# Rotary embedding on one core: six slabs in flight, engine passes of 2048 elements

## Chip, cores and metric

The kernel runs on one core of a Trainium2 chip. The metric is the time of the program on the device in microseconds (us), the median of several runs. Beside it stands one execution taken by the hardware profiler, with its own span from the first to the last instruction.

Five kinds of engine matter here. VectorE (DVE in the profile) does the multiplications and additions, ScalarE (ACT) the conversions between float32 and bf16, TensorE (PE) and GpSimd (POOL) a little preparation. SyncE (SP), ACT and POOL also issue transfers between the memory outside (HBM) and the on-chip memory of 128 partitions. Each of these three has a queue of its own, and all queues are worked off by the core's 16 DMA engines.

## What is computed

The input x has 16 batches of 512 positions with 16 heads of 64 elements. In each head the first 32 elements and the last 32 are rotated against each other by a cosine and a sine of the position (float32 in and out, 33.5 MB each way):

```python
x = x.reshape(batch, seq, num_heads, head_dim)        # 16, 512, 16, 64
x1, x2 = x[..., :half_dim], x[..., half_dim:]
cos = cos[None, :, None, :]                           # cos, sin: 512 x 32
sin = sin[None, :, None, :]
rotated = np.concatenate([x1 * cos - x2 * sin,
                          x1 * sin + x2 * cos], axis=-1)
```

## The kernel before

The work is cut into 8 slabs (`nslabs`) of two batches. A slab is one tile of 128 partitions with 8192 float32 each (8 positions of 1024 elements, `rpp = 8`), 32 KB in a partition and 4 MB in all. One transfer loads it, and one stores it from the same tile. The pool `slabs` has 5 such tiles (`slots`), so a load of slab s + 5 can only start when the store of slab s has landed.

*Loads* (L60 to L64). Slab 0 is issued on SP, then the two tables cos and sin (L73), then slabs 1 to 4. Further loads are issued in the main loop behind the store of the slab whose tile they take: slab 5 still on SP, slabs 6 and 7 on POOL (`s < nslabs - 2` chooses). SP has nothing else to do; POOL has only the preparation at the start, so a wait in front of a load holds up nothing else there.

*Tables* (L80 to L103). GpSimd builds a selection matrix and converts the tables to bf16, four matmuls spread them to 128 partitions, and VectorE copies the result to `tab`: a cosine part, and a sine part with signs.

*Passes.* A pass (s, r, n) is n of the 8 positions of slab s, that is n x 1024 elements in each partition. Slabs 1 to 5 are one pass of 8192 elements, slabs 0, 6 and 7 two passes of 4096. A pass goes through:

1. `cast` (L112): ScalarE copies the float32 slab to the bf16 buffer `xb`. There are two such buffers (`xpool`), each as large as a whole slab in bf16 (16 KB in a partition).
2. VectorE multiplies twice (L133), by the sine part into `t2` and by the cosine part in place. `t2` lies in the slab's own memory, whose float32 values are no longer needed.
3. VectorE adds the two, with the halves of each head exchanged (L136).
4. ScalarE copies the bf16 result back to the slab as float32 (L139).
5. Behind the last pass of a slab ScalarE issues the store (L141).

The loop casts one pass ahead: on ScalarE the cast of pass i + 1 comes in front of the copy back of pass i. An engine works in the order of its instructions, so where that cast waits for a slab still to be loaded, the copy back and the store behind it wait too. The scheduler of the language reorders within this: at the start, it puts the cast of slab 1 in front of both copies back of slab 0, and it interleaves the VectorE operations of the first two passes.

Of the kernel before, what the change touches and what calls it, by code (L numbers as in the profile page):

```python
# [2 lines left out]

# [4 lines left out]


@with_exitstack  # L10
def kernel(
    ctx: ExitStack,
    tc: tile.TileContext,
    x: bass.AP,
    cos: bass.AP,
    sin: bass.AP,
    num_heads: int,
    out: bass.AP,
):
    nc = tc.nc  # L20
    P = nc.NUM_PARTITIONS

    batch, seq, dim = x.shape
    nh = num_heads
    hd = dim // nh
    half = hd // 2
    bf16 = mybir.dt.bfloat16
    f32 = mybir.dt.float32

    nb = 2  # L30
    slots = 5
    nslabs = batch // nb
    rpp = nb * seq // P
    W = rpp * dim
    SP = seq // rpp
    TW = rpp * half

    out_flat = out.rearrange("b s h d -> b s (h d)")

    singles = ctx.enter_context(tc.tile_pool(name="singles", bufs=1))  # L40
    slabs = ctx.enter_context(tc.tile_pool(name="slabs", bufs=slots))
    xpool = ctx.enter_context(tc.tile_pool(name="xpool", bufs=2))
    psum = ctx.enter_context(tc.tile_pool(
        name="psum", bufs=1, space=bass.MemoryType.PSUM))


    def dram(t, s, a=0, n=W):
        return bass.AP(tensor=t.tensor, offset=t.offset + s * nb * seq * dim + a,
                       ap=[[W, P], [1, n]])


    def view(t, offset, *dims):
        return dataclasses.replace(t, offset=t.offset + offset,
                                   ap=[t.ap[0], *[list(d) for d in dims]])


    slab = {}


    def load(s):  # L60

        queue = nc.sync if s < nslabs - 2 else nc.gpsimd
        slab[s] = slabs.tile([P, W], f32, tag="slab", name="slab")
        queue.dma_start(out=slab[s], in_=dram(x, s))  # L64


    load(0)


    cos_sb = singles.tile([SP, TW], f32, tag="cos_sb")  # L70
    sin_sb = singles.tile([SP, TW], f32, tag="sin_sb")
    for t, src in ((cos_sb, cos), (sin_sb, sin)):
        nc.sync.dma_start(out=t, in_=bass.AP(  # L73
            tensor=src.tensor, offset=src.offset, ap=[[TW, SP], [1, TW]]))

    for s in range(1, slots):
        load(s)

    pick = singles.tile([SP, 2 * P], bf16, tag="pick")
    nc.gpsimd.memset(pick, 0.0)  # L82
    for g in range(2):
        part = view(pick, g * P, (SP, P // SP), (1, SP))
        nc.gpsimd.affine_select(  # L85
            out=part, in_=part, compare_op=mybir.AluOpType.not_equal,
            fill=1.0 - 2.0 * g, base=0, pattern=[[0, P // SP], [-1, SP]],
            channel_multiplier=1)

    tab1 = singles.tile([SP, 2 * TW], bf16, tag="tab1")  # L90
    for i, t in enumerate((cos_sb, sin_sb)):
        nc.gpsimd.tensor_copy(out=view(tab1, i * TW, (1, TW)), in_=t)  # L92

    acc = psum.tile([P, 2 * rpp * hd], f32, tag="acc")
    for i in range(2):
        for h in range(2):
            nc.tensor.matmul(  # L97
                view(acc, i * rpp * hd + h * half, (hd, rpp), (1, half)),
                view(pick, i * h * P, (1, P)),
                view(tab1, i * TW, (half, rpp), (1, half)),  # L100
                start=True, stop=True)
    tab = singles.tile([P, 2 * rpp * hd], bf16, tag="tab")
    nc.vector.tensor_copy(out=tab, in_=acc)  # L103

    xb = {}


    def cast(u):
        s, r, n = u
        if r == 0:  # L110
            xb[s] = xpool.tile([P, W], bf16, tag="xb", name="xb")
        nc.scalar.copy(out=view(xb[s], r * dim, (1, n * dim)),  # L112
                       in_=view(slab[s], r * dim, (1, n * dim)))

    passes = []
    for s in range(nslabs):
        n = rpp if 1 <= s < nslabs - 2 else rpp // 2  # L120
        passes += [(s, r, n) for r in range(0, rpp, n)]


    cast(passes[0])
    for i, (s, r, n) in enumerate(passes):
        if i + 1 < len(passes):
            cast(passes[i + 1])
        xs = view(slab[s], r * dim, (1, n * dim))
        xu = view(xb[s], r * dim, (1, n * dim))

        t2 = view(slab[s].bitcast(bf16), 2 * r * dim, (1, n * dim))
        for t, a in ((t2, rpp * hd), (xu, 0)):
            nc.vector.tensor_mul(  # L133
                out=t, in0=xu,
                in1=view(tab, a + r * hd, (hd, n), (0, nh), (1, hd)))
        nc.vector.tensor_add(  # L136
            out=xu, in0=xu, in1=view(t2, half, (hd, n * nh), (-half, 2), (1, half)))

        nc.scalar.copy(out=xs, in_=xu)  # L139
        if r + n == rpp:  # L140
            nc.scalar.dma_start(out=dram(out_flat, s), in_=slab[s])  # L141
            if s + slots < nslabs:
                load(s + slots)


# [1 line left out]
_INS = ['x', 'cos', 'sin', 'num_heads']  # L147
_OUTS = [((16, 512, 16, 64), 'float32')]

_NUMBERS = {'num_heads': 16}  # L150


# [26 lines left out]
```

## Time and profile before

| What | Value |
|---|---|
| Median of 3 runs | 162.46 us (162.06 to 162.85) |
| Span of the profiled execution | 160.2 us |
| DVE busy | 108.6 us (68%) |
| ACT busy | 113.5 us (71%) |
| Bytes moved by DMA | 67.24 MB, mean 420 GB/s over the span |
| Loads on SP | 6, median 26.6 us from issue to landing |
| Loads on POOL | 2, median 24.9 us |
| Stores on ACT | 8, median 25.9 us |

The slices in the profile are fortieths of the span, 4 us each; a digit is the busy share of a slice in tenths, and 9 stands for 90% or more. A line of an instruction group has the source line, the engine, the operation, output and inputs with their shapes, the count; then the busy time and the mean length of one in ns; then the idle time of the engine just before these instructions and what ended it. A line of the timeline has the start, the length, the engine, the source line and the operation; a bracket has the idle time before it and what ended that. An engine named with a q (SPq, ACTq) is its instruction queue: issuing a transfer takes time there and is not counted as busy.

### The profile page before, as it was taken

What the parts mean: (1) busy time and instruction counts of PE and PEld (TensorE: products, weight loads), DVE (VectorE), ACT (ScalarE), POOL (GpSimd) and SP (SyncE); (2) the same over time, 40 slices, a digit from 0 to 9 for tenths busy, and PEclk for the clock granted to TensorE, in tenths of its full rate; (3) what the DMA queues carried; (4) which work ended last, traced back from release to release, by engine and by line L of the source; (5) the groups of instructions that cost most, each with busy time, mean ns of one, the idle gap of its engine ahead of it and who ended that gap; (6) DMA issues with size and microseconds to landing.
All of it is one profiled execution on the core that took longest, in us unless ns stands there. A gap on an engine that the chain in (4) does not pass through costs nothing.

```text
span 160.2 us, 159 instructions
## 1 busy us (share of the span) xinstructions
PE 1.0 (1%) x4; PEld 0.5 (0%) x4; DVE 108.6 (68%) x34; ACT 113.5 (71%) x23; POOL 3.0 (2%) x11
## 2 busy tenths in 40 slices
PE   0002000000000000000000000000000000000000
PEld 0000000000000000000000000000000000000000
DVE  0001899999979979997997299919839499940000
ACT  3006929998999999899919995089995999553000
POOL 2001000000000000000010001000000000000000
DMA  7999999999999999999999999999999999999995
GB/s 246 409 393 426 393 450 466 393 417 491 401 393 426 491 393 409 499 401 393 483 434 393 450 466 393 426 483 401 409 491 409 393 475 442 393 442 475 393 426 229
DMA packets 2464, 67.24 MB, mean 420 GB/s; under 512 B 288, under 2 KB 416, under 8 KB 416
## 3 DMA queue, kind: packets, MB, share of 16 engines
q10 hardware_dynamic: 1152, 33.55, 48.5%
q1 hardware_dynamic: 1024, 25.30, 37.5%
q0 software_dynamic: 288, 8.39, 12.1%
HBM read 33.69 MB, written 33.55 MB: 420 GB/s over the span
## 4 chain that ended last, share of the span: by engine, by line
DMA 49%; ACT 28%; issue 8%; DVE 4%; SPq 1%; ACTq 0%; POOLq 0%
DMA slab<-in_x_dram 29%; DMA out_dram<-slab 20%; ACT slab L139 16%; ACT xb L112 12%; DVE xb L136 1%; DVE xb L133 1%; DVE slab L133 1%; SPq L73 1%; ACTq L141 0%; SPq L64 0%; POOLq L174 0%; ACTq L139 0%; POOLq L64 0%
## 5 line engine op out<-in xcount | busy, mean ns | idle before, releaser
L112 ACT CAST xb<-slab 128x4096 bf16<-128x4096 f32 (+1 forms) x11 | 56.6, 5155 | 27.8 <-DMA slab<-in_x_dram 26.5
L139 ACT CAST slab<-xb 128x4096 f32<-128x4096 bf16 (+1 forms) x11 | 56.6, 5154 | 3.5 <-DVE xb L136 3.5
L133 DVE TENSOR_TENSOR slab<-xb,tab 128x4096 bf16<-128x4096 bf16 (+1 forms) x11 | 35.9, 3260 | 17.3 <-ACT xb L112 17.2
L133 DVE TENSOR_TENSOR xb<-xb,tab 128x4096 bf16<-128x4096 bf16 (+1 forms) x11 | 35.9, 3261 | 0.3
L136 DVE TENSOR_TENSOR xb<-xb,slab 128x4096 bf16<-128x4096 bf16 (+1 forms) x11 | 35.9, 3261 | 0.3
L103 DVE CAST tab<-acc 128x1024 bf16<-128x1024 f32 x1 | 1.2, 1225 | 15.2 <-PE acc L97 15.2
L64 POOL DMA_DIRECT2D slab<-in_x_dram x2 | 1.2, 608 | 84.1 <-DMA out_dram<-slab 84.1
L112 ACT ACT_TABLE_LOAD x1 | 1.3, 1283 | 0.7 <-PEq L160 0.7
L97 PE MATMUL acc<-tab,pick 64*128 64x256 bf16 x4 | 1.0, 402 | 14.2 <-POOL tab L92 14.2
L92 POOL CAST tab<-cos_sb 64x256 bf16<-64x256 f32 x1 | 0.4, 389 | 12.1 <-DMA cos_sb<-in_cos_dram 12.1
L85 POOL TENSOR_SCALAR_AFFINE_SELECT pick<-pick 64x128 bf16<-64x128 bf16 x2 | 0.5, 285 | 0.1
L97 PEld LDWEIGHTS <-pick 64*128 64x128 bf16 x4 | 0.5, 122 | 14.2 <-issue 12.6
L92 POOL CAST tab<-sin_sb 64x256 bf16<-64x256 f32 x1 | 0.4, 394 | 0.0
L82 POOL MEMSET pick<- 64x256 bf16 x1 | 0.3, 304 | 0.3 <-POOLq L160 0.3
L160 POOL MEMSET const-float32-0.0<- 128x1 f32 x1 | 0.1, 103 | 0.2 <-issue 0.2
L160 POOL MEMSET const-bfloat16-1.0<- 128x1 bf16 x1 | 0.1, 107 | 0.0
L160 POOL MEMSET const-uint8-127<- 128x1 uint8 x1 | 0.1, 106 | 0.0
L160 POOL MEMSET const-float32-1.0<- 128x1 f32 x1 | 0.1, 103 | 0.0
## 6 DMA issues: line engine op xcount, KB each, us to landing
out_dram<-slab ACTq DMA_DIRECT2D x8, 4096.0 KB, 25.9
slab<-in_x_dram SPq DMA_DIRECT2D x6, 4096.0 KB, 26.6
slab<-in_x_dram POOLq DMA_DIRECT2D x2, 4096.0 KB, 24.9
cos_sb<-in_cos_dram SPq DMA_DIRECT2D x1, 64.0 KB, 12.5
sin_sb<-in_sin_dram SPq DMA_DIRECT2D x1, 64.0 KB, 12.3
```

Source lines behind the costliest of these rows:

```text
L64: queue.dma_start(out=slab[s], in_=dram(x, s))
L73: nc.sync.dma_start(out=t, in_=bass.AP(tensor=src.tensor, offset=src.offset, ap=[[TW, SP], [1, TW]]))
L82: nc.gpsimd.memset(pick, 0.0)
L85: nc.gpsimd.affine_select(out=part, in_=part, compare_op=mybir.AluOpType.not_equal, fill=1.0 - 2.0 * g, base=0, pattern=[[0, P // SP], [-1 ...
L92: nc.gpsimd.tensor_copy(out=view(tab1, i * TW, (1, TW)), in_=t)
L97: nc.tensor.matmul(view(acc, i * rpp * hd + h * half, (hd, rpp), (1, half)), view(pick, i * h * P, (1, P)), view(tab1, i * TW, (half, rpp) ...
L103: nc.vector.tensor_copy(out=tab, in_=acc)
L112: nc.scalar.copy(out=view(xb[s], r * dim, (1, n * dim)), in_=view(slab[s], r * dim, (1, n * dim)))
L133: nc.vector.tensor_mul(out=t, in0=xu, in1=view(tab, a + r * hd, (hd, n), (0, nh), (1, hd)))
L136: nc.vector.tensor_add(out=xu, in0=xu, in1=view(t2, half, (hd, n * nh), (-half, 2), (1, half)))
L139: nc.scalar.copy(out=xs, in_=xu)
L160: nc = _bacc.Bacc("TRN2", target_bir_lowering=False, num_devices=1)
```

## The change

Three things are changed. The pool has six slab tiles instead of five; slabs 0 to 5 are loaded on SP, 6 and 7 on POOL, which the line that chooses the queue now says with `slots`. The bf16 buffers hold one pass instead of one slab (two of 2048 elements, 4 KB in a partition, in place of two of 16 KB), and are taken anew for each pass. Each of the 8 slabs goes through the engines in four passes of 2048 elements, 32 passes in place of 11.

```diff
-    slots = 5
+    slots = 6
...
     def load(s):
 
-        queue = nc.sync if s < nslabs - 2 else nc.gpsimd
+        queue = nc.sync if s < slots else nc.gpsimd
...
     def cast(u):
         s, r, n = u
-        if r == 0:
-            xb[s] = xpool.tile([P, W], bf16, tag="xb", name="xb")
-        nc.scalar.copy(out=view(xb[s], r * dim, (1, n * dim)),
-                       in_=view(slab[s], r * dim, (1, n * dim)))
+        xb[u] = xpool.tile([P, n * dim], bf16, tag="xb", name="xb")
+        nc.scalar.copy(out=xb[u], in_=view(slab[s], r * dim, (1, n * dim)))
...
     for s in range(nslabs):
-        n = rpp if 1 <= s < nslabs - 2 else rpp // 2
+        n = rpp // 4
         passes += [(s, r, n) for r in range(0, rpp, n)]
...
         xs = view(slab[s], r * dim, (1, n * dim))
-        xu = view(xb[s], r * dim, (1, n * dim))
+        xu = xb[s, r, n]
```

With 32 passes there are 32 casts, 32 copies back and 96 operations on VectorE, where there were 11, 11 and 33. The order on ScalarE is now a strict exchange: cast of pass i + 1, copy back of pass i, with the store issued behind the fourth copy back of a slab. A cast takes the buffer that the copy back just ahead of it has read. The first load in the loop, that of slab 6, waits for the store of slab 0, and that of slab 7 for the store of slab 1; the number and size of all transfers are as before.

## The prediction

> **What bounds the kernel now.** I read the slices and the queue table first, then the windows at both ends, then the instruction groups with shapes kept apart, then the timeline, and last the records that the trace keeps of every DMA packet. The slices and the queue table:
>
> ```profile
> span 160.2 us, 159 instructions
> ...
> DMA  7999999999999999999999999999999999999995
> ...
> q10 hardware_dynamic: 1152, 33.55, 48.5%
> q1 hardware_dynamic: 1024, 25.30, 37.5%
> q0 software_dynamic: 288, 8.39, 12.1%
> ```
>
> Between the first and the last slice the 16 DMA engines never fall below nine tenths, and the three queues (q1 is SP's loads, q10 ACT's stores, q0 POOL's loads) add up to 98.1% of their time. The windows at the ends show where the rest is:
>
> ```profile
> 0.00:2.40 2.40, 0.00 (x0) 0.10 (x1) 0.00 (x0) 1.28 (x1) 1.05 (x7) 1.00 0.72 191
> ...
> 157.00:160.20 3.20, 0.00 (x0) 0.00 (x0) 0.00 (x0) 0.00 (x0) 0.00 (x0) 1.00 0.38 164
> ```
>
> The last two columns are the DMA share and GB/s. So DMA is idle only while the first transfer is set up and while the last store completes. The kernel is bound by 16 slab transfers (8 in, 8 out). A packet is one partition's 32768 bytes, each engine moves 8 of them for a slab, and a packet takes 1.216 us: a slab alone is 8 x 1.216 = 9.73 us, and two queues that are busy together each take 19.4 us for one (the packet records have slab 4's load from 44.1 to 63.5, beside the stores).
>
> The engines are the second limit:
>
> ```profile
> L112 ACT CAST xb<-slab 128x8192 bf16<-128x8192 f32 x5 | 35.1, 7018 | 7.9 <-DMA slab<-in_x_dram 6.6 <-ACT slab L139 1.3
> ...
> L139 ACT CAST slab<-xb 128x4096 f32<-128x4096 bf16 x6 | 21.5, 3602 | 3.5 <-DVE xb L136 3.5
> ...
> L133 DVE TENSOR_TENSOR slab<-xb,tab 128x8192 bf16<-128x8192 bf16 x5 | 22.1, 4425 | 7.3 <-ACT xb L112 7.3
> ...
> L133 DVE TENSOR_TENSOR xb<-xb,tab 128x4096 bf16<-128x4096 bf16 x6 | 13.7, 2291 | 0.2
> ```
>
> The rates fix the short forms. ScalarE: (7018 - 3602) / 4096 = 0.834 ns an element, and 186 ns fixed. VectorE: (4425 - 2291) / 4096 = 0.521 ns an element, and 157 ns fixed. The timeline gives the moments that the change touches:
>
> ```profile
> 13.38 7.11 ACT L112 CAST xb<-slab 128x4096 bf16<-128x4096 f32 x2 [11.37 <-DMA slab<-in_x_dram]
> ...
> 37.60 0.38 ACTq L141 DMA_DIRECT2D out_dram<-slab  x1
> ...
> 79.90 0.69 POOL L64 DMA_DIRECT2D slab<-in_x_dram  x1 [65.41 <-DMA out_dram<-slab]
> ...
> 99.23 0.53 POOL L64 DMA_DIRECT2D slab<-in_x_dram  x1 [18.65 <-DMA out_dram<-slab]
> ...
> 145.54 0.34 ACTq L141 DMA_DIRECT2D out_dram<-slab  x1
> ```
>
> Stores issue about every 14.4 us, the loads of slabs 6 and 7 wait on POOL for the stores of slabs 1 and 2, and the last store issues at 145.5 us while earlier stores still move: its own first packet starts only at 148.9 us, its last ends at 159.2. The engines thus have some 3 us in hand.
>
> **The change, part by part.** *Bytes and transfers* are the same 16 slabs, so the DMA time itself (156.7 us of packets per engine) is neither removed nor shortened. With no idle in the middle, deeper buffering has nothing to fill. The kernel can stay at 160.2 us or lose.
>
> The Trainium skill says the same of queues in "DMA: Bandwidth & Descriptors", Rules for kernel authors: spreading transfers over SP, ACT and GpSimd brings no bandwidth, as all run on the same 16 engines. In this trace SP alone moved 431 GB/s (23 to 37.6 us), and SP and ACT together 433 (60 to 80).
>
> *Shorter passes.* A 2048-element copy is 186 + 2048 x 0.834 = 1.894 us, a multiply or add 157 + 2048 x 0.521 = 1.224. Between them lie 0.02 us (ScalarE behind its own result, read at 51.97 to 51.99), 0.035 (VectorE behind its own), 0.03 (copy to VectorE, 91.23 to 91.26) and 0.05 (VectorE to copy; the one case in the trace is 0.09 with two waits). With two xb buffers the way from one VectorE pass to the second next is: copy out, copy in, three VectorE operations: 0.05 + 1.894 + 0.02 + 1.894 + 0.03 + 3 x 1.224 + 2 x 0.035 = 7.63 us for two passes, 15.25 for a slab. Behind each slab ScalarE also issues a store (0.38 more, on this way): **15.63 us a slab**, against 14.35 now (store issues at 51.99 and 66.34). Bounds: ScalarE's own work, 8 x 1.894 + 0.40 less four overlaps of 0.09 and plus 0.08, is 15.27; with every hand-over at 0.09 the sum is about 16.2.
>
> The Trainium skill, "VectorE: DVE Perf Modes", The TRN2 errata, charges each instruction a fixed part that small tiles pay per tile, 58 cycles at 0.96 GHz for VectorE: an estimate of 1.127 us for this operation. The rows measure 157 ns fixed instead of 60, so the measurement decides; by the page ScalarE would set the period at 15.3 us, and the sum below would end at 160.4 us instead of 161.5.
>
> *First store.* Slab 0 lands at 13.4 and the tables at 16.5, as now. The first two passes are interleaved on VectorE (six operations from 16.5 end at 23.65). On ScalarE: out 0 from 21.3, in 2, out 1 (to 26.9), in 3 (to 28.8), out 2 (28.9 to 30.8), the first piece of slab 1 (landed at 23.8, so no wait; to 32.7), out 3 to 34.6. Store 0 issues at **34.6 us instead of 37.6**, and, if no load is waited for, the last one at 34.6 + 7 x 15.63 = 144.0.
>
> *Six slabs.* SP now issues loads 0 to 5 at once; the wait that goes is this one:
>
> ```profile
> SPq L64 <- DMA out_dram<-slab: 56.7, 1, 56.7
> ```
>
> The sixth load has one wait left, for a semaphore that the cos table used (landed at 13.7 us); its turn in the ring comes 40 us later, so this costs nothing. Loads 6 and 7 stay on POOL, but wait for stores 0 and 1. So where load 6 came after load 5, it now starts while loads 4 and 5 are still queued on SP: a **third busy queue**, which takes its share from the slabs that are needed sooner. By the packet records, step by step:
>
> - Store 0's first packet came 3.7 us after its issue (37.60 to 41.26): now 38.3. Load 2 ends at 33.0 as before, so load 3 is 5.3 us in.
> - Two queues share evenly until store 0 lands: 38.3 + 19.5 + 0.3 = 58.1. From a store's landing to the first packet of the load that it frees on POOL took 5.5 us (79.3 to 84.8; 98.7 to 104.2): load 6 starts at 63.6.
> - By then SP has moved 5.3 + 25.3/2 = 17.95 of the 29.2 us of loads 3 to 5; 11.25 are left. At a third each they take 33.7 us, to 97.3. The other two queues stay busy so long: load 6 takes 29.2 us to 92.8, load 7 is behind it (store 1 lands near 83), and stores 1 to 3 issue at 50, 66 and 81.
> - A slab has landed when the slowest engine is done. In turns of three its last packet can lie up to two packet times (2.4 us) behind the even share; I take 1.2, and 0.3 for the landing: **slab 5 is there at 98.8 us**. Nothing here shows three queues, so: with no loss to the third (SP keeps half) it would be 87.6, with POOL taking half 100.3. I take a third, as the two queues of today share evenly.
>
> Store 4 stands behind slab 5's first copy on ScalarE, and would be ready at 97.1; it now issues at 98.8 + 2 x 1.9 = 102.6. Behind it come three slabs of engine work, 3 x 15.63 = 46.9: the last store issues at 149.5. DMA has nothing else to do from 149.5 on (the other 15 slabs end there), so this is a tail with nothing over it: 1.24 to the first packet (as load 0, 0.74 to 1.98), 9.73 to move, 0.97 to the end of the span (159.18 to 160.15). **Sum: 149.5 + 11.9 = 161.5 us, 1.3 more than 160.2.** The median of the runs, 162.46, lies 2.3 above the profiled span, so 163.8.
>
> The bounds: slowest engine 0 to 2.4 us (-1.2 to +1.2); period 15.27 to 16.2 (-1.1 to +1.7); POOL taking half, +1.5; store 0's first packet only 1.24 us after issue, as on idle engines, which moves load 6 forward and slab 5 to 103.7, +4.9. Downward everything stops at the DMA floor of 160.2.
>
> **Rivals.** *The floor holds (not slower).* If slab 5 lands by 97.4, the last store issues before 148.2 and is hidden behind the store before it. Then the span stays at 160.2 and the time at 162.4. For it: 1.4 us decide, and the bounds reach that far. Against it: it needs every hand-over as short as its best row.
>
> *The engine loop becomes the bound.* If the exchange between ScalarE and VectorE costs 0.3 us more a pass, a slab takes 16.83. Store 4 issues at 34.6 + 4 x 16.83 = 101.9 by the loop alone, at 102.6 by slab 5, so both end together, and the last store is at 102.6 + 50.5 = 153.1: 165.0 us, a time of 167.3. For it: 42 more ScalarE instructions, each waiting on the other engine with only two buffers. Against: today's hand-overs are 0.03 to 0.09.
>
> *Faster.* The packets exceed 128 x 1.213 by 1.4 us (slow ones at 2, 13 and 41 us). If an earlier store avoids those but the first, at most 0.9 us go: 161.5. Nothing in the change touches their cause.
>
> **How the numbers follow.** The late slab 5 has 0.56 (of which 0.06 ends within 0.5%), the floor 0.27, the engine loop 0.11, faster 0.06. 0.5%, 0.8 us, is about what a measurement of this kernel tells from no change. So slower 0.61, same 0.33, faster 0.06. The predicted time is the first case's, 163.8; the range runs from 162.0 (the floor, with the 0.4 us by which the runs spread) to 168.0 (the bounds upward together less their least likely part).
>
> **What would show it.** Right: ScalarE's 2048 forms at 1.89 us, store 0 near 34.6, a long wait of ScalarE for slab 5's load of some 5 us near 94 to 99, load 6 landing before load 5, three engine-bound slabs after it, and a dip in the DMA row near 149. Wrong: no dip (the floor), ScalarE waiting mainly for VectorE in every pass (the loop), or slab 5 landing before 93.

## The result and the profile after

The changed kernel takes 163.56 us (median of 12 runs, 162.61 to 164.28) beside 162.72 us for the kernel before, run on the same chip. The ratio is 1.0067, with a 95% interval from 1.0041 to 1.0092: slower by two thirds of a percent. The prediction was 163.8. The profiled span went from 160.2 to 161.8 us. Some executions, of the kernel before too, are 2 to 5 us longer; the ratios leave them out, while 162.72 is the median of all 12.

These are the page's lines of the kernel after: the span, the DMA row in 40 slices, the queues, and the groups of the two engines.

```profile
span 161.8 us, 266 instructions
...
DMA  7999999999999899999899999999999999996996
...
q10 hardware_dynamic: 1152, 33.55, 48.1%
q1 hardware_dynamic: 1024, 25.30, 37.2%
q0 software_dynamic: 288, 8.39, 12.0%
q14 instruction: 2, 0.02, 0.0%
...
L111 ACT CAST xb<-slab 128x2048 bf16<-128x2048 f32 x32 | 60.6, 1898 | 20.5 <-DMA slab<-in_x_dram 16.9
L137 ACT CAST slab<-xb 128x2048 f32<-128x2048 bf16 x32 | 60.7, 1896 | 7.6 <-DVE xb L134 6.5
L131 DVE TENSOR_TENSOR slab<-xb,tab 128x2048 bf16<-128x2048 bf16 x32 | 39.2, 1225 | 11.6 <-ACT xb L111 11.5
```

The DMA row has a 6 in the slice from 145.6 to 149.7 us, which it did not have before. The short copies take 1.90 us and the short multiplications 1.225. The three queues of data moved the same bytes, and the slab packets took 156.8 us an engine against 156.7 before: DMA did not become slower. One line is new, q14, two packets that carry instructions; it comes back below.

The timeline of the kernel after shows the store issues, the two loads on POOL, and the wait for slab 5 (lines of the same engine around them left out):

```profile
35.12 0.37 ACTq L139 DMA_DIRECT2D out_dram<-slab  x1
...
59.37 0.69 POOL L64 DMA_DIRECT2D slab<-in_x_dram  x1 [44.48 <-ACT slab L137]
...
99.06 1.90 ACT L111 CAST xb<-slab 128x2048 bf16<-128x2048 f32 x1 [5.22 <-DMA slab<-in_x_dram]
...
102.79 0.34 ACTq L139 DMA_DIRECT2D out_dram<-slab  x1
...
118.44 0.34 ACTq L139 DMA_DIRECT2D out_dram<-slab  x1
...
134.10 0.34 ACTq L139 DMA_DIRECT2D out_dram<-slab  x1
...
149.81 0.34 ACTq L139 DMA_DIRECT2D out_dram<-slab  x1
```

ScalarE stands 5.2 us before slab 5's first copy. From there the stores issue at nearly even distances of 15.65 to 15.71 us, that is, at the pace of the engines. (The bracket of the POOL load names ScalarE as the last releaser; it waits for the store of slab 0 as well, whose landing is complete at 58.7 us in the trace.) The windows around the last store have the DMA share and GB/s in their last two columns:

```profile
146.00:148.00 2.00, 0.00 (x0) 0.00 (x0) 1.76 (x2) 0.12 (x1) 0.00 (x0) 1.00 1.14 492
148.00:149.00 1.00, 0.00 (x0) 0.00 (x0) 0.00 (x0) 1.00 (x1) 0.00 (x0) 1.00 0.23 98
149.00:150.00 1.00, 0.00 (x0) 0.00 (x0) 0.00 (x0) 0.78 (x1) 0.00 (x0) 1.00 0.01 0
150.00:151.00 1.00, 0.00 (x0) 0.00 (x0) 0.00 (x0) 0.00 (x0) 0.00 (x0) 1.00 1.22 524
```

A packet counts where it starts, so a share can exceed 1. No packet of data starts between 149 and 150 us, while ScalarE is still copying the last pass (0.78 us busy). By the packet records every engine stands still for 0.75 to 2.05 us there, 25.6 us over the 16, or 1.6 us each; that is the whole growth of the span. (The records do not name the engine of a packet; here and below a packet that starts where another ends is taken to be on the same engine. Their times are given on the axis of the timeline.)

### The profile page after: what moved, and what is told of

Its sections match the earlier page's. It is cut to its first block, busy times and chain, and to the rows that moved or that the text cites. A ratio compares the mean times of both kernels' runs of the same rounds, so it can differ in the third digit from the quotient of the medians.

```text
span 161.8 us, 266 instructions
## 1 busy us (share of the span) xinstructions
PE 1.0 (1%) x4; PEld 0.5 (0%) x4; DVE 118.4 (73%) x97; ACT 121.0 (75%) x65; POOL 3.0 (2%) x11
## 4 chain that ended last, share of the span: by engine, by line
ACT 41%; DVE 36%; DMA 8%; another core or an unknown queue 3%; issue 2%; ACTq 2%; PE 1%; POOL 0%; SPq 0%; DVEq 0%
ACT slab L137 21%; ACT xb L111 20%; DVE slab L131 12%; DVE xb L131 11%; DVE xb L134 11%; DMA cos_sb<-in_cos_dram 8%; ACTq L139 1%; DVE tab L103 1%; PE acc L97 1%; POOL tab L92 0%; SPq L64 0%; DVEq L131 0%; ACTq L137 0%; ACTq L111 0%
## 5 line engine op out<-in xcount | busy, mean ns | idle before, releaser
L111 ACT CAST xb<-slab 128x2048 bf16<-128x2048 f32 x32 | 60.6, 1898 | 20.5 <-DMA slab<-in_x_dram 16.9
L137 ACT CAST slab<-xb 128x2048 f32<-128x2048 bf16 x32 | 60.7, 1896 | 7.6 <-DVE xb L134 6.5
L131 DVE TENSOR_TENSOR slab<-xb,tab 128x2048 bf16<-128x2048 bf16 x32 | 39.2, 1225 | 11.6 <-ACT xb L111 11.5
L131 DVE TENSOR_TENSOR xb<-xb,tab 128x2048 bf16<-128x2048 bf16 x32 | 39.2, 1224 | 1.1
L134 DVE TENSOR_TENSOR xb<-xb,slab 128x2048 bf16<-128x2048 bf16 x32 | 39.2, 1225 | 1.1
```

The costliest lines, as they stand in the source:

```text
L111: nc.scalar.copy(out=xb[u], in_=view(slab[s], r * dim, (1, n * dim)))
L131: nc.vector.tensor_mul(out=t, in0=xu, in1=view(tab, a + r * hd, (hd, n), (0, nh), (1, hd)))
L134: nc.vector.tensor_add(out=xu, in0=xu, in1=view(t2, half, (hd, n * nh), (-half, 2), (1, half)))
```

## The experiments

Each experiment has its own runs of the kernel before on its chip; the ratios are against those.

**All loads on SP.** Slabs 6 and 7 queue up behind slab 5 instead of running beside it.

```diff
-        queue = nc.sync if s < slots else nc.gpsimd
+        queue = nc.sync
```

> All eight loads on SP, otherwise the changed kernel. Theory (a third busy queue delays slab 5, and the last three slabs end as a tail of the engines): load 5 lands near 87 us instead of 98.8, slabs 6 and 7 near 107 and 126, just ahead of or about 1 us behind their turn; the last store issues near 145 and is hidden behind the store before it; no dip in the DMA row near 149; span 160.3, ratio to the kernel before 1.000 (0.998 to 1.002). Rival (short passes cost the time by themselves): span 161.8 and ratio 1.007 stay.

Measured: 162.66 us, ratio 1.0036 (1.0024 to 1.0048), span 160.8. The only wait for a load behind the start, and the last store:

```profile
126.08 1.90 ACT L111 CAST xb<-slab 128x2048 bf16<-128x2048 f32 x1 [0.91 <-DMA slab<-in_x_dram]
...
145.52 0.34 ACTq L139 DMA_DIRECT2D out_dram<-slab  x1
```

and the same windows as above:

```profile
148.00:149.00 1.00, 0.00 (x0) 0.00 (x0) 0.00 (x0) 0.00 (x0) 0.00 (x0) 1.00 0.76 328
149.00:150.00 1.00, 0.00 (x0) 0.00 (x0) 0.00 (x0) 0.00 (x0) 0.00 (x0) 1.00 0.84 360
```

Slab 5 has landed at 87.3 instead of 99.0 us, ScalarE's wait of 5.2 us is gone, the last store issues 4.3 us earlier and the gap in DMA is closed (the kernel before has 0.61 and 0.84 in these two windows). This is one changed word in the queue, with the same passes and buffers: the late slab comes from the third queue. But the span ends at 160.8 and not at 160.3, and the interval excludes 1.000. About half a microsecond is left that the theory did not have. (The intervals of this ratio and of the changed kernel's touch, 1.0041 to 1.0048; the wait, the store and the gap tell the two apart.)

**The short passes alone.** Five slabs and the loads of the kernel before, with four passes.

```diff
-    slots = 6
+    slots = 5
...
-        queue = nc.sync if s < slots else nc.gpsimd
+        queue = nc.sync if s < nslabs - 2 else nc.gpsimd
```

> Four passes and the small bf16 buffers alone: five slabs, loads 6 and 7 on POOL and load 5 on SP as in the kernel before. Theory: passes take 15.7 us a slab, but never more than two queues are busy, no slab is late by more than 1 us, the last store issues near 145; span 160.3, ratio 1.000. Rival (short passes cost the time by themselves): 161.8 and 1.007.

Measured: 162.53 us, ratio 1.0021 (1.0002 to 1.0040), span 160.7. The last store issues at 144.4 us and no slab is waited for in the middle. Neither expectation holds exactly: the passes do not cost the 1.6 us, but a small rest again remains, about the same as with all loads on SP. Slabs 6 and 7 are loaded on POOL here too; with five tiles load 6 issues at 77.5 us and not at 59.4, and no slab is late. So what counts is when POOL's queue is busy, not that it is used.

**The third queue moved by one slab.** Slab 6 goes behind slab 5 on SP, slab 7 alone on POOL.

```diff
-        queue = nc.sync if s < slots else nc.gpsimd
+        queue = nc.sync if s < nslabs - 1 else nc.gpsimd
```

> Load 6 goes on SP behind load 5, load 7 alone stays on POOL, where it starts once store 1 has landed (near 84 us). Theory: the third queue now delays slab 6 and not slab 5: load 5 lands near 88, load 7 near 113, load 6 only near 118; the cast of slab 6 waits some 8 us, two slabs of engine work and a store follow: the last store issues near 153, span 164.9 (163.5 to 166), ratio 1.03, although fewer loads run beside SP's. Rival (short passes): 161.8, ratio 1.007. Rival (cost grows with the number of loads on POOL): between 160.2 and 161.8.

Measured: 165.92 us, ratio 1.0236 (1.0212 to 1.0260), span 163.9.

```profile
116.64 1.90 ACT L111 CAST xb<-slab 128x2048 bf16<-128x2048 f32 x1 [7.69 <-DMA slab<-in_x_dram]
...
151.74 0.34 ACTq L139 DMA_DIRECT2D out_dram<-slab  x1
```

With one load less on POOL the kernel gets slower, because the victim is now slab 6, with two slabs of engine work behind it. This tells "which slab is overtaken" from "how many loads run on POOL". The wait is 7.7 us, about as expected. It ends at 116.6 us where slab 6 was expected near 118, and the last store issues at 151.7 where 153 was expected; the span is inside the expected range.

**Engine work added to the tail.** One more ScalarE copy in each of slabs 5, 6 and 7, once in the changed kernel and once with all loads on SP.

```diff
+    pad = singles.tile([P, 768], bf16, tag="pad")
...
         nc.scalar.copy(out=xs, in_=xu)
+        if s >= 5 and r == 0:
+            nc.scalar.copy(out=pad, in_=view(xu, 0, (1, 768)))
```

> The changed kernel with one more ScalarE copy of 768 elements (186 + 768 x 0.834 = 827 ns) in each of slabs 5, 6 and 7, read from the pass just done, so that it stays in its place; its output is stored nowhere. Theory (the end is a tail of the engines behind slab 5): ScalarE and VectorE take between 0.45 and 0.83 us more a slab, so the last store issues 1.3 to 2.5 us later than 149.8 and the span is 163.1 to 164.3, ratio 1.015 to 1.023. Rival (DMA moves slower with three queues, the engines have time): 161.8 and 1.007 stay.

> The same extra copies with all loads on SP. Theory: the last store issues 1.3 to 2.5 us later than 145.5, still while the store before it moves, so nothing is seen: span 160.8, ratio 1.0036 as without the copies (within 0.002). Rival (engine time always shows): 1.3 us or more later, ratio 1.012 to 1.019.

Measured in the changed kernel: 165.74 us, ratio 1.0205 (1.0179 to 1.0230), span 164.0. With all loads on SP: 162.57 us, ratio 1.0024 (1.0004 to 1.0044), span 160.8. The store issues of the first one after slab 5's wait:

```profile
99.55 1.90 ACT L112 CAST xb<-slab 128x2048 bf16<-128x2048 f32 x1 [5.92 <-DMA slab<-in_x_dram]
...
103.28 0.34 ACTq L142 DMA_DIRECT2D out_dram<-slab  x1
...
119.50 0.34 ACTq L142 DMA_DIRECT2D out_dram<-slab  x1
...
151.99 0.34 ACTq L142 DMA_DIRECT2D out_dram<-slab  x1
```

and the last store of the second:

```profile
146.12 0.34 ACTq L142 DMA_DIRECT2D out_dram<-slab  x1
```

The first distance between stores is 119.50 - 103.28 = 16.22 us, 0.57 more than without the copy. In the first kernel the last store issues 2.2 us later than without the copies: 1.7 are the three copies, and 0.5 is slab 5, whose first copy starts at 99.55 instead of 99.06 in this execution. All of it shows in the span (+2.2). In the second kernel the last store issues only 0.6 us later, not the 1.3 to 2.5 expected, mainly because the wait of 0.9 us for slab 7 takes up part of the added work and is gone; nothing of the 0.6 shows in the span. So behind the late slab 5 the end is engine time, and without the late slab the store in front covers it.

A first form of this experiment read nothing from the slabs.

```diff
+            nc.scalar.copy(out=pad, in_=pad_in)
```

> The changed kernel with one more ScalarE copy of 512 elements (0.61 us) in each of slabs 5, 6 and 7, which computes nothing that is stored. Theory (the end is a tail of the engines): 3 x 0.6 us more, span 163.7, ratio 1.018 (1.014 to 1.022). Rival (the end is set by DMA, which only moves slower with three queues): no more than 161.8 and 1.007.

Measured: 165.97 us, ratio 1.0243 (1.0182 to 1.0304). It tells nothing. The scheduler moved all three copies to the start, so slabs 5 to 7 had no more work than before (the last store issued at 148.1 us), and in its profile one of the 16 DMA engines ended at 162.9 us, the others by 159.4; the records have stores' packets of 1.7 to 1.9 us between 51 and 72 us. All six runs took 165.0 us or more; why is open.

**The half microsecond.** In both versions without a late slab two packets of 8192 bytes on q14, the queue of instructions, fall into the run. In the version with all loads on SP they start at 83.5 and 111.5 us; the packet behind each takes 1.84 and 1.52 us instead of 1.21; and the two engines that took them are the last to end, at 159.42 and 159.35 us; the others, but for one at 159.2, have ended by 158.9. With the short passes alone they start at 83.6 and 102.9 us, the packets behind them take 1.75 and 1.33, and the two engines end at 159.5 and 159.0, the others by 158.8. The kernel before has no such packet in the run, and its last engine ends at 158.9. Three kernels were to test whether the longer program is the cause: two lengthen the program of the kernel before, one splits the passes less far. The first puts instructions that nothing uses in front of the copy of the tables:

```diff
+    spare = singles.tile([P, 8], bf16, tag="spare")
+    for _ in range(64):
+        nc.vector.memset(spare, 0.0)
```

> The kernel before with 64 more VectorE memsets of 8 bf16 elements at the start, while VectorE waits for the tables anyway. Theory on the 0.5 us that the versions with four passes lose without any late slab (the longer program is itself fetched by DMA packets of 8192 bytes in the middle of the run, and the slowest engine sets the end): one or two such packets appear, the packet behind each takes about 1.8 instead of 1.2 us, the slowest engine ends near 159.7 instead of 159.2, span 160.7, ratio 1.002 to 1.003. Rival (the short passes' own work does it): no change, 160.2 and 1.000.

Measured: 166.44 us (162.90 to 166.88), without a ratio. In its profile one DMA engine ends at 162.8 us and the others by 161.0; the one packet of instructions comes early, at 10.1 us. Inconclusive.

The second has five slabs, the loads of the kernel before, and two passes a slab (the last line of the edit; the others are those of the short passes alone):

```diff
-        n = rpp // 4
+        n = rpp // 2
```

> Five slabs, loads as in the kernel before, two passes of 4096 elements for every slab with small buffers. Theory on the 0.5 us: with 48 VectorE operations in place of 96 fewer or no program packets fall into the run (none, or one); a slab takes about 14.9 us, so no late slab; span 160.2 to 160.4, ratio 0.999 to 1.0015. Rival (any split into shorter passes costs 0.5 us): 160.7, 1.003.

Measured: 162.36 us, ratio 1.0017 (0.9984 to 1.0050), span 160.5, no packet of instructions before the last store has landed.

The third stands behind the loop of the kernel before, under its last store:

```diff
+    spare = singles.tile([P, 8], bf16, tag="spare")
+    for _ in range(64):
+        nc.vector.tensor_copy(out=spare, in_=view(xu, 0, (1, 8)))
```

> The kernel before with 64 VectorE copies of 8 elements behind the last addition, under the last store; their output is stored nowhere. All transfers, passes and buffers are those of before. Theory on the 0.5 us (program packets of a longer program): one or two packets of 8192 bytes of the instruction kind appear during the run, the engine that takes one is the slowest at the end (near 159.7 instead of 159.2), span 160.6 to 160.9, ratio 1.002 to 1.003, and no run as short as the shortest of before. Rival (the short passes' own work): 160.2, ratio 1.000, shortest runs equal.

Measured: 162.97 us, ratio 1.0014 (0.9989 to 1.0040), span 161.4, above the 160.6 to 160.9 expected. The queue table of this kernel has the line that the kernel before lacks:

```profile
q14 instruction: 1, 0.01, 0.0%
```

The packet starts at 147.3 us, the one behind it takes 1.57 us, and that engine ends at 160.1, last of the 16 together with one other, which took none. In this execution nearly every engine also has a packet of 1.4 to 1.95 us between 95 and 98 us, so it does not single out the packet of instructions. The shortest run is 162.45 us, beside 161.96 of the kernel before; the shortest with two passes was 161.99, with four passes 162.38 to 162.49. The shortest runs thus part by the presence of these packets, as the theory says, but the intervals of the last two experiments hold both expectations. That a program packet delays its engine is seen in the traces; that it makes the whole half microsecond is likely and not settled.

## Why the prediction was right

The sum came out right, 161.5 us for a span of 161.8, and so did the path: the late slab 5, three slabs at the engines' pace behind it, and a last store with nothing over it. One part of it agrees by luck, and one term was missing.

- *Nothing to gain.* The sum held that DMA has no idle time in the middle and that its floor stays. Packet time was 156.8 us an engine against 156.7, and no version went below the kernel before.
- *Pass and period.* 1.894 and 1.224 us were expected, 1.898 and 1.225 came; 15.63 us a slab against 15.65 between the store issues at 102.79 and 118.44. That the exchange between ScalarE and VectorE sets the period, and not ScalarE alone with 15.3, was right. The chain that ended last goes to and fro between the two, with 7.64 us from 105.10 to 112.74 for two passes, where 7.63 was expected (start, length, engine and line):

```profile
105.10 1.24 DVE slab L131
...
107.62 1.24 DVE xb L134
108.88 1.91 ACT slab L137
110.81 1.91 ACT xb L111
112.74 1.24 DVE slab L131
```

- *First store.* 34.6 expected, 35.1 measured: slab 0 and the tables arrived 0.3 to 0.5 us later in this execution.
- *Slab 5.* The even third was the one step without a row. It held: between 65 and 90 us the queues of SP, ACT and POOL started 110, 106 and 118 slab packets. Load 6's first packet came at 64.05 us (63.6 expected). Slab 5 had landed at 99.0 and its first copy started at 99.06 (98.8 expected), but by a different split, and that is luck: its last packet of data ended at 96.1, some 1 us before the even share at 97.3, and 2.8 us lay from there to the landing, where the prediction had 1.2 for the slowest engine and 0.3 for the landing. An engine reports that its part is done with a packet of 4 bytes in the same queue, and this packet takes its turn too: where the data ended at 96.14 the report came at 98.56, behind one packet of each other queue.
- *Axis of the packets.* The prediction gives times of packets 0.24 us later than the timeline and the windows have them: the last slab packet of the kernel before ends at 158.94, not 159.18. So a store's first packet came 3.4 us after its issue and not 3.7, a load's 5.3 us after the landing that freed its tile and not 5.5, and of the 11.9 us of the tail 1.0 stand ahead of the first packet and 1.2 behind the last, not 1.24 and 0.97. The tail's sum stays.
- *Tail.* Last store 149.5 expected, 149.8 measured; from there 12.0 us to the end, 11.9 expected. The two experiments with added copies show that this tail is engine time with nothing over it.
- *The floor.* Here a term was missing. The rival "the floor holds" was put at the old span, 160.2 us; the two versions that reach it end at 160.7 and 160.8. So by the spans a late slab 5 costs 1.0 us over a version without it (by the ratios, 1.0067 against 1.0036 and 1.0021, 0.5 to 0.75), and some 0.5 us would have come anyway, with the longer program as the likely cause. In the changed kernel that half microsecond is hidden: all engines stand idle near 149 us, so an engine that is late by 0.9 us catches up there.

The rival of the engine loop fell with the period, 15.65 us a slab and not 16.83; the short passes alone give 160.7 us. The rival of a gain fell with the packet time.

## What to carry to other kernels

Where DMA is busy throughout, as here, a deeper buffer moves no byte sooner; it only changes which transfer is served when. A load on a queue of its own overtakes those that wait in another queue, so a prefetch that is needed late belongs behind the loads that are needed first, in their queue. And the engine time of work that is split finer is hidden only as long as the last transfer is issued before the one in front of it ends: look at the time between the two, here 3 us, before spending it.

## What was not expected

- Four passes nearly triple the number of VectorE and ScalarE instructions (34 to 97 and 23 to 65), and the program itself then comes through the same 16 DMA engines in the middle of the run: two packets of 0.31 us, each with a slow packet behind it (1.3 to 1.9 us instead of 1.21).
- With three queues busy the reports of the 16 engines for one load came over 3.0 us (95.6 to 98.6), with two queues over 1.9 (84.9 to 86.8, all loads on SP). A report can wait for a packet of each other busy queue: two of them, 2.4 us, in the example above; one, 1.2 us, on an engine where all loads are on SP (data to 84.64, report at 85.83). A transfer is as late as its last report, so this time belongs into a sum beside the share of the data.
